# Layer 0's head norms: the Newton steps of a reciprocal square root, moved from VectorE to GpSimd

## The chip, the cores and the metric

The kernel runs on one core of a Trainium2 chip. A core has five engines that run side by side, each with its own in-order queue: TensorE (matrix products; PE in the profile, PEld for its weight loads), VectorE (DVE), ScalarE (ACT), GpSimd (POOL) and SyncE (SP, which here issues the loads). They wait for each other through semaphores. The metric is the time of one execution on the device in microseconds (us), lower is better.

## The reference, cut to what matters

Two transformer layers on 512 tokens of width 2048. Layer 0 is differential attention with 8 heads; layer 1 is another attention and has no head norm. What is computed around the change:

```python
o = from_blocks(lax.map(block, (to_blocks(q), jnp.arange(S // BLOCK))))   # (B, S, 8 heads, 256)
o = rms_norm(o, subln_g) * (1.0 - lam_init)
o = o.reshape(B, S, A_WIDTH) * jax.nn.silu(g)
return o @ w_out

def rms_norm(x, g):
    xf = x.astype(jnp.float32)
    y = xf * lax.rsqrt(jnp.mean(jnp.square(xf), axis=-1, keepdims=True) + EPS)
    return (y * g.astype(jnp.float32)).astype(x.dtype)
```

So each token of each head needs one reciprocal square root of its mean square over 256 values.

## The kernel before, in words

Activations and weights are fp32, held as a high part and a low part (`hh`/`hl`, `whi`/`wlo`); each product is three matmuls: L173 high x high, L174, L175 (with a low part). Weights stream from HBM into `wst`; ScalarE rounds a piece to `whi` (L93) and VectorE makes `wlo` (L94), some pieces ahead of use. A projection is a `group`: eight pieces of two 128-row tiles, each multiplied into four accumulator banks `acc`, so 24 matmuls per piece. A "burst" is six of these.

Attention of a head is cut into pieces, and one is issued after every burst of a projection (`tick`), so that TensorE has projection work while the vector engines work on the head. For layer 0 the attention of head h-1 runs beside the projections of head h. Its pieces, per block of 128 tokens i (0 to 3): two `score` (matmuls into `sc`; VectorE's L699 adds the bias and finds the row's extreme; ScalarE's exponential L703; VectorE's L707 to L711 combine both components into `e`), `turn` (TensorE transposes `e`, L720; the result is split into `ah` and `al`, L168 and L169), `values` (matmuls into `o`), and after every second `values` a `norm`, for two token blocks at once. `store` later transposes `og` on TensorE (L767), and ScalarE copies it out (L769). The order of pieces after the scores: values(1) with the first norm, score(3,0), turn(2), score(3,1), an empty one, values(2), store(0), turn(3), store(1), values(3) with the second norm, four empty ones, store(2), store(3). So a head has a first and a second norm, 16 norms in layer 0.

A norm: ScalarE copies `o` to `og` (L746) and sums the squares into `ss`, 128 tokens x 2 blocks (L749). VectorE scales `ss` (L750) and calls `rsqrt` on the 128x2 values: a first guess by integer operations (L246, L247, the latter writing `rstd`), the halved argument (L248), then three Newton steps of three instructions (L253, L254, L255). Then two instructions L753 multiply `og` by `rstd` and by the gate `sg`. `rsqrt` with n == 1 serves the layer norms, with two instructions a step (L251, L255). `rsqrt` with n == 2 is used by these 16 norms alone.

VectorE also carries, beside this, the sums of the modulation vectors: `macc` (L386), fed by loads `ms`, and turned into rows by two matmuls (L406, L407). At the end of a projection of values and gates it frees the accumulator banks (`vl`, L169, and `sg`, L675).

Only the start of the program has a written order. From there on a scheduler orders each engine's queue by its own estimates, so a changed instruction can move others. GpSimd has had little to do: the constants at the start, and `dist` (L646).

Of the kernel before, what the change touches and what calls it, by code (L numbers as in the profile page):

```python
# [13 lines left out]
ALU = mybir.AluOpType  # L14
# [95 lines left out]
def tile_yoco(  # L110
# [24 lines left out]
    V, S, PE, G = nc.vector, nc.scalar, nc.tensor, nc.gpsimd  # L135
# [105 lines left out]
    def rsqrt(y, v, n, pool):  # L241

        t = pool.tile([P, n], I32, name="rs_t", tag=f"rs_t{n}", bufs=2)
        a = pool.tile([P, n], F32, name="rs_a", tag=f"rs_a{n}", bufs=2)
        h = pool.tile([P, n], F32, name="rs_h", tag=f"rs_h{n}", bufs=2)
        V.tensor_scalar(t, v.bitcast(I32), 1, None, op0=ALU.logical_shift_right)  # L246
        V.tensor_scalar(y.bitcast(I32), t, -1.0, float(0x5F3759DF), op0=ALU.mult, op1=ALU.add)  # L247
        V.tensor_scalar(h, v, -0.5, None, op0=ALU.mult)  # L248
        for _ in range(3):
            if n == 1:  # L250
                V.scalar_tensor_tensor(a, y, h, y, op0=ALU.mult, op1=ALU.mult)  # L251
            else:
                V.tensor_tensor(a, y, y, op=ALU.mult)  # L253
                V.tensor_tensor(a, a, h, op=ALU.mult)  # L254
            V.scalar_tensor_tensor(y, a, 1.5, y, op0=ALU.add, op1=ALU.mult)  # L255


    ws = WeightStream(nc, wpool)
# [419 lines left out]
    def attention_a(h, lead=3, late=()):  # L678
# [62 lines left out]
        def norm(p):  # L741
            o = st["o", p]
            og = ap.tile([P, 2, 256], F32, name="og", tag="og", bufs=1)
            ss = ap.tile([P, 2], F32, name="ss", tag="ss", bufs=2)
            rstd = ap.tile([P, 2], F32, name="rstd", tag="rstd", bufs=2)
            S.copy(og.rearrange("p r e -> p (r e)"), o)  # L746
            for r in range(2):
                orow = o[:, r * 256 : (r + 1) * 256]
                S.activation(orow, orow, AF.Square, accum_out=ss[:, r : r + 1])  # L749
            V.tensor_scalar(ss, ss, 1.0 / 256.0, EPS, op0=ALU.mult, op1=ALU.add)  # L750
            rsqrt(rstd, ss, 2, ap)
            for r in range(2):
                V.scalar_tensor_tensor(  # L753
                    og[:, r, :], og[:, r, :], rstd[:, r : r + 1], cur[h, "sg"][:, 2 * p + r, :],
                    op0=ALU.mult, op1=ALU.mult,
                )
            st["og", p] = og
# [83 lines left out]
    def moments(pool, stats, b):  # L841
        mv = pool.tile([P, 2], F32, name="mv", tag="mv", bufs=4)
        V.bn_aggr(mv, stats[:, b, :, :])
        ve = pool.tile([P, 1], F32, name="lve", tag="lve", bufs=4)
        rstd = pool.tile([P, 1], F32, name="lrstd", tag="lrstd", bufs=4)
        V.tensor_scalar(ve, mv[:, 1:2], EPS, None, op0=ALU.add)
        rsqrt(rstd, ve, 1, pool)
        return mv, rstd
# [450 lines left out]
```

## Time and profile before

| | |
|---|---|
| median of 3 runs | 2016.16 us (2014.56 to 2017.47) |
| profiled execution | 2017.03 us, span of its profile 2015.2 us |
| mean granted TensorE clock | 0.995 |
| layer 0's norms | from 248 to 871 us |

The span is what lies between the first and the last instruction in the profile; the time of an execution is a little longer. Shares of busy time are means over stages with different limits. In lists of instructions each row has the start, the time taken, engine, line, operation, result and operands, form, and, in brackets, how long the engine sat idle before it and what released it. In a table of waits a row has the waiting engine and line, what it waited for, the total, the number of times and the longest. In the view of one tile a row has the shortest, median and longest time in ns.

### The profile page before, as it was taken

What the parts mean: (1) busy time and instruction counts of PE and PEld (TensorE: products, weight loads), DVE (VectorE), ACT (ScalarE), POOL (GpSimd) and SP (SyncE); (2) the same over time, 40 slices, a digit from 0 to 9 for tenths busy, and PEclk for the clock granted to TensorE, in tenths of its full rate; (3) what the DMA queues carried; (4) which work ended last, traced back from release to release, by engine and by line L of the source; (5) the groups of instructions that cost most, each with busy time, mean ns of one, the idle gap of its engine ahead of it and who ended that gap; (6) DMA issues with size and microseconds to landing.
All of it is one profiled execution on the core that took longest, in us unless ns stands there. A gap on an engine that the chain in (4) does not pass through costs nothing.

```text
span 2015.2 us, 25053 instructions
## 1 busy us (share of the span) xinstructions
PE 1966.7 (98%) x9115; PEld 1624.6 (81%) x9115; DVE 1334.4 (66%) x2435; ACT 722.3 (36%) x1230; POOL 2.2 (0%) x10
## 2 busy tenths in 40 slices
PE   5999999999999999999999999999999999999997
PEld 4888878888878888888878877888888888888885
DVE  7887878777667677753575666645455555576678
ACT  2423444433333334432273222224333333453232
POOL 0000000000000000000000000000000000000000
PEclk8999999999999999999999999999999999999998
DMA  9995755574556565552344878844233323333754
GB/s 342 346 314 149 238 174 162 166 222 156 190 166 210 160 225 178 162 165 94 115 144 135 268 252 260 259 123 129 90 104 95 104 90 104 95 117 93 259 191 177
DMA packets 263095, 353.79 MB, mean 176 GB/s; under 512 B 18022, under 2 KB 162556, under 8 KB 262204
## 3 DMA queue, kind: packets, MB, share of 16 engines
q1 hardware_dynamic: 260592, 347.99, 53.7%
q10 hardware_dynamic: 2380, 4.21, 0.6%
q8 instruction: 71, 1.16, 0.2%
q14 instruction: 52, 0.43, 0.1%
HBM read 339.47 MB, written 12.66 MB: 175 GB/s over the span
## 4 chain that ended last, share of the span: by engine, by line
PE 77%; DVE 10%; DMA 10%; issue 2%; ACT 1%; SPq 1%; DVEq 0%; ACTq 0%
PE acc L173 22%; PE acc L175 22%; PE acc L174 22%; DMA ms<-in_w_mod_dram 7%; DVE macc L386 3%; DVE wlo L94 2%; PE sc L173 2%; PE sc L174 2%; PE sc L175 1%; DMA ms<-in_kv_w_mod_dram 1%; PE o L175 1%; PE o L174 1%; PE o L173 1%; PE tr L1163 1%; DMA sms<-in_w_mod_dram 1%
## 5 line engine op out<-in xcount | busy, mean ns | idle before, releaser
L93 ACT CAST whi<-wst 128x1024 fp32r<-128x1024 f32 (+2 forms) x339 | 349.5, 1032 | 672.9 <-PE acc L175 281.6
L94 DVE TENSOR_TENSOR wlo<-wst,whi 128x1024 fp32r<-128x1024 f32 (+2 forms) x339 | 404.4, 1195 | 268.1 <-ACT whi L93 263.9
L173 PE MATMUL acc<-whi,hh 128*128 128x512 f32 x1252 | 492.6, 397 | 0.9 <-ACT hh L933 0.8
L174 PE MATMUL acc<-wlo,hh 128*128 128x512 f32 x1252 | 489.7, 391 | 2.6 <-DVE wlo L94 2.6
L175 PE MATMUL acc<-whi,hl 128*128 128x512 f32 x1252 | 488.1, 390 | 0.0
L173 PE MATMUL acc<-hh,whi 128*128 128x512 f32 x1184 | 468.5, 396 | 1.3 <-ACT vt L977 0.9
L175 PE MATMUL acc<-hh,wlo 128*128 128x512 f32 x1184 | 462.3, 390 | 2.0 <-DVE wlo L94 2.0
L174 PE MATMUL acc<-hl,whi 128*128 128x512 f32 x1184 | 461.7, 390 | 0.0
L386 DVE SCALAR_TENSOR_TENSOR macc<-ms,cact,macc 128x512 f32<-128x512 f32 x360 | 269.9, 750 | 128.4 <-DMA ms<-in_w_mod_dram 95.6
L175 PEld LDWEIGHTS acc<-whi,hl 128*128 128x128 f32 x1252 | 235.3, 188 | 50.8 <-DVE hl L934 0.3
L174 PEld LDWEIGHTS acc<-wlo,hh 128*128 128x128 f32 x1252 | 235.6, 188 | 47.8 <-DVE wlo L94 4.3
L173 PEld LDWEIGHTS acc<-whi,hh 128*128 128x128 f32 x1252 | 235.7, 188 | 46.8 <-ACT hh L933 1.2
L175 PEld LDWEIGHTS acc<-hh,wlo 128*128 128x128 f32 x1184 | 222.3, 188 | 52.2 <-DVE wlo L94 4.2
L173 PEld LDWEIGHTS acc<-hh,whi 128*128 128x128 f32 x1184 | 222.5, 188 | 45.7 <-ACT vt L977 1.7
L174 PEld LDWEIGHTS acc<-hl,whi 128*128 128x128 f32 x1184 | 222.6, 188 | 41.1
L476 DVE SCALAR_TENSOR_TENSOR sacc<-sms,cact,sacc 128x512 f32<-128x512 f32 (+1 forms) x127 | 89.5, 705 | 4.8 <-DMA sms<-in_w_mod_dram 1.2
L1152 ACT ACTIVATE eb<-eb,mnb 128x128 f32<-128x128 f32 (+1 forms) x64 | 36.1, 563 | 96.4 <-DVE mnb L1149 95.2
L703 ACT ACTIVATE e<-e,mn 128x128 f32<-128x128 f32 (+3 forms) x64 | 36.0, 563 | 89.5 <-DVE mn L699 88.7
L1149 DVE CUSTOM_DVE_ANT_0 eb<-sc,biasb 128x128 f32<-128x128 f32 (+1 forms) x64 | 31.3, 490 | 52.7 <-PE sc L175 52.7
L1167 DVE TENSOR_TENSOR pTl<-tr,pTh 128x128 fp32r<-128x128 f32 (+1 forms) x64 | 31.2, 487 | 26.5 <-ACT pTh L1166 26.2
L1166 ACT CAST pTh<-tr 128x128 fp32r<-128x128 f32 (+1 forms) x64 | 27.2, 424 | 43.6 <-PE tr L1163 43.1
L769 ACT ACTIVATE ogT<-tr,subg 128x128 f32<-128x128 f32 x64 | 20.0, 364 | 56.4 <-PE tr L767 56.4
(251 smaller groups left out, 1739.2 us busy)
## 6 DMA issues: line engine op xcount, KB each, us to landing
wst<-in_a_w_in_dram SPq DMA_DIRECT2D x240, 256.0 KB
ms<-in_w_mod_dram SPq DMA_DIRECT2D x64, 512.0 KB
ms<-in_kv_w_mod_dram SPq DMA_DIRECT2D x64, 512.0 KB
wst<-in_kv_w_dram SPq DMA_DIRECT2D x64, 512.0 KB
ms<-in_w_mod_dram SPq DMA_DIRECT2D x128, 256.0 KB
wst<-in_b_w_in_dram SPq DMA_DIRECT2D x128, 256.0 KB
sms<-in_w_mod_dram SPq DMA_DIRECT2D x56, 512.0 KB
wst<-in_b_w_out_dram SPq DMA_DIRECT2D x48, 512.0 KB
```

Source lines behind the costliest of these rows:

```text
L93: self.nc.scalar.copy(hi[:, :, :w], st[:, :, :w])
L94: self.nc.vector.tensor_tensor(lo[:, :, :w], st[:, :, :w], hi[:, :, :w].bitcast(F32), op=ALU.subtract)
L173: PE.matmul(dst, lhs[0], rhs[0], start=start, stop=False)
L174: PE.matmul(dst, lhs[0], rhs[1], start=False, stop=False)
L175: PE.matmul(dst, lhs[1], rhs[0], start=False, stop=stop)
L386: V.scalar_tensor_tensor(acc, w, cact[:, kt : kt + 1], acc, op0=ALU.mult, op1=ALU.add)
L476: V.scalar_tensor_tensor(acc, w, sc, acc, op0=ALU.mult, op1=ALU.add)
L703: S.activation(e[:, :w], e[:, :w], AF.Exp, bias=mn, scale=-1.0, accum_out=rs)
L1149: V.tensor_tensor_reduce(out=e[:, :w], in0=sc[:, :w], in1=bias[:, :w], scale=-1.0, scalar=3.0e38, op0=ALU.add, op1=ALU.min, accum_out=mn)
L1152: S.activation(e[:, :w], e[:, :w], AF.Exp, bias=mn, scale=-1.0, accum_out=rs)
L1166: S.copy(pTh[:, 0 : i + 1, ts], src)
L1167: V.tensor_tensor(pTl[:, 0 : i + 1, ts], src, pTh[:, 0 : i + 1, ts].bitcast(F32), op=ALU.subtract)
```

## The change

In `rsqrt`, where n is not 1, the Newton steps go to GpSimd. The fused last instruction of a step (add 1.5, multiply) becomes two, so a step has four instructions and a norm twelve, each waiting for the one before. The first guess and the halved argument stay on VectorE, and so do the two multiplications after the root. The root of the layer norms (n == 1) is as it was.

```diff
         for _ in range(3):
             if n == 1:
                 V.scalar_tensor_tensor(a, y, h, y, op0=ALU.mult, op1=ALU.mult)
+                V.scalar_tensor_tensor(y, a, 1.5, y, op0=ALU.add, op1=ALU.mult)
             else:
-                V.tensor_tensor(a, y, y, op=ALU.mult)
-                V.tensor_tensor(a, a, h, op=ALU.mult)
-            V.scalar_tensor_tensor(y, a, 1.5, y, op0=ALU.add, op1=ALU.mult)
+
+                G.tensor_tensor(a, y, y, op=ALU.mult)
+                G.tensor_tensor(a, a, h, op=ALU.mult)
+                G.tensor_scalar(a, a, 1.5, None, op0=ALU.add)
+                G.tensor_tensor(y, a, y, op=ALU.mult)
```

Lines behind this place have numbers three higher in the changed kernel.

On VectorE, head 0's first norm, the old order with - and the new with +, from the first guess on:

```order
 L247 TENSOR_SCALAR rstd<-rs_t 128x2
-L657 SCALAR_TENSOR_TENSOR q0l<-part,q0h 128x512
-L253 TENSOR_TENSOR rs_a<-rstd 128x2
+L660 SCALAR_TENSOR_TENSOR q0l<-part,q0h 128x512
 L169 TENSOR_TENSOR k0l<-part,k0h 128x512
-L254 TENSOR_TENSOR rs_a<-rs_a,rs_h 128x2
+L389 SCALAR_TENSOR_TENSOR macc<-ms,cact,macc 128x512
+L756 SCALAR_TENSOR_TENSOR og<-og,rstd,sg 128x256 x2
 L169 TENSOR_TENSOR al<-tr,ah 128x384
```

Here `og` moved: before, 13 other instructions stood between the guess and it, with the nine Newton instructions strewn among them; now three do, and `al`, the next scores and `wlo` follow it.

On VectorE, head 2's second norm, where nothing else stood between (before, from the guess on):

```order
L247 TENSOR_SCALAR rstd<-rs_t 128x2
L253 TENSOR_TENSOR rs_a<-rstd 128x2
L254 TENSOR_TENSOR rs_a<-rs_a,rs_h 128x2
L255 SCALAR_TENSOR_TENSOR rstd<-rs_a,rstd 128x2
L253 TENSOR_TENSOR rs_a<-rstd 128x2
L254 TENSOR_TENSOR rs_a<-rs_a,rs_h 128x2
L255 SCALAR_TENSOR_TENSOR rstd<-rs_a,rstd 128x2
L253 TENSOR_TENSOR rs_a<-rstd 128x2
L254 TENSOR_TENSOR rs_a<-rs_a,rs_h 128x2
L255 SCALAR_TENSOR_TENSOR rstd<-rs_a,rstd 128x2
L753 SCALAR_TENSOR_TENSOR og<-og,rstd,sg 128x256 x2
```

And the same place now:

```order
L247 TENSOR_SCALAR rstd<-rs_t 128x2
L756 SCALAR_TENSOR_TENSOR og<-og,rstd,sg 128x256 x2
L94 TENSOR_TENSOR wlo<-wst,whi 128x1024
L169 TENSOR_TENSOR vl<-acc,vh 128x256 x2
L678 SCALAR_TENSOR_TENSOR sg<-th,acc 128x256 x2
```

The nine instructions are gone, and `og`, which waits for GpSimd, is the next in the queue; the weight split and the freeing of the banks stand behind it as before.

On TensorE, head 1's second norm, the transposes of `og` in the first bursts after it, now:

```order
L173 MATMUL acc<-whi,hh 128x512
L174 MATMUL acc<-wlo,hh 128x512
L770 MATMUL tr<-ident,og 128x128 x2
L175 MATMUL acc<-whi,hl 128x512
L173 MATMUL acc<-whi,hh 128x512
L174 MATMUL acc<-wlo,hh 128x512
L175 MATMUL acc<-whi,hl 128x512
L770 MATMUL tr<-ident,og 128x128 x2
L173 MATMUL acc<-whi,hh 128x512
L174 MATMUL acc<-wlo,hh 128x512
L175 MATMUL acc<-whi,hl 128x512
```

Both pairs moved ahead of 15 matmuls that stood before them; before, the second pair was followed by one more burst's three matmuls and head 2's first score:

```order
L174 MATMUL acc<-wlo,hh 128x512
L767 MATMUL tr<-ident,og 128x128 x2
L175 MATMUL acc<-whi,hl 128x512
L173 MATMUL acc<-whi,hh 128x512
L174 MATMUL acc<-wlo,hh 128x512
L175 MATMUL acc<-whi,hl 128x512
L767 MATMUL tr<-ident,og 128x128 x2
L173 MATMUL acc<-whi,hh 128x512
L174 MATMUL acc<-wlo,hh 128x512
L175 MATMUL acc<-whi,hl 128x512
L173 MATMUL sc<-k0h,q0h 128x256
```

At head 0's and head 4's second norms they moved ahead by one burst or less. On TensorE nothing else moved but the two matmuls of a modulation row at head 1's second norm. SP's loads of heads 0 and 1 changed places among themselves.

## The prediction

> **What bounds the kernel now.** I read the page's busy times first, then the stage of the head norms by itself (240 to 880 us, columns as in the table of stages: span, then busy time and count for PE, PEld, DVE, ACT, POOL, the granted clock, the DMA share, GB/s), then what TensorE waited for in that stage.
>
> ```profile
> span 2015.2 us, 25053 instructions
> PE 1966.7 (98%) x9115; PEld 1624.6 (81%) x9115; DVE 1334.4 (66%) x2435; ACT 722.3 (36%) x1230; POOL 2.2 (0%) x10
> 240.00:880.00 640.00, 633.47 (x3002) 525.45 (x3001) 457.21 (x974) 251.98 (x513) 0.00 (x0) 1.00 0.57 181
> PE tr L767 <- DVE og L753: 4.4, 5, 1.3
> PE tr L767 <- DVE al L169: 0.9, 1, 0.9
> PE tr L720 <- DVE ss L750: 0.6, 1, 0.6
> ```
>
> TensorE bounds it. In the 640 us of this stage it idles 640 - 633.5 = 6.5 us, at a granted clock of 1.00; VectorE is busy 457 us, 71%. So less work on VectorE is worth nothing by itself. Only two things count: how early a result that TensorE waits for comes, and how long VectorE's queue stands. The last three rows name 5.9 of those 6.5 us, and the largest, 4.4 us in five waits, ends with `og`, the instruction fed by the root that is moved. They are at head 0's two norms, head 1's first, head 4's second and head 5's first. No row names a load: the order of the weight and modulation loads on SP's queue, which shifts a little in heads 0 and 1, I cost at nothing, covered by TensorE's 24-matmul steps per loaded piece. Were that cover gone, a load would appear among these waits.
>
> **What is removed.** Nine VectorE instructions per norm, 16 norms: 144.
>
> ```profile
> L94 DVE TENSOR_TENSOR wlo<-wst,whi 128x1024 fp32r<-128x1024 f32 (+2 forms) x339 | 404.4, 1195 | 268.1 <-ACT whi L93 263.9
> L253 DVE TENSOR_TENSOR rs_a<-rstd x48: 141/161/164, 250.2 to 869.8; 128x2 f32<-128x2 f32 x48
> 381.93 0.17 DVE L247 TENSOR_SCALAR rstd<-rs_t 128x2 int32<-128x2 int32 x1
> 383.98 0.88 DVE L753 SCALAR_TENSOR_TENSOR og<-og,rstd,sg 128x256 f32<-128x256 f32 x2
> 386.51 0.38 PE L767 MATMUL tr<-ident,og 128*128 128x128 f32 x2
> 386.78 0.75 DVE L675 SCALAR_TENSOR_TENSOR sg<-th,acc 128x256 f32<-128x256 f32 x2
> 388.27 0.48 PE L173 MATMUL acc<-hh,whi 128*128 128x512 f32 x1
> 389.05 0.40 PE L173 MATMUL acc<-hh,whi 128*128 128x512 f32 x1
> 389.74 0.39 PE L173 MATMUL acc<-hh,whi 128*128 128x512 f32 x1
> ```
>
> The first Newton line (L253) takes 0.16 us, the median of 48, and the other two the same. 144 x 0.16 = 23 us of VectorE busy time go; off TensorE's path, so worth 0. The timeline rows are head 2's second norm, where the nine run alone: from the end of L247 (382.10) to `og` (383.98) they take 1.88 us, about 0.2 each. The new chain has to be held against 1.88 us there, and against 5 to 7 us where other work was interleaved.
>
> **What is added.** Twelve GpSimd instructions per norm, each waiting for the one before, with a handover from VectorE and one back. No row shows such an instruction on GpSimd; the nearest are its start-up rows:
>
> ```profile
> 0.24 0.10 POOL L1286 MEMSET const-float32-0.0<- 128x1 f32 x1 [0.24 <-issue]
> 0.87 0.20 POOL L181 MEMSET ones<- 128x128 f32 x1
> 1.11 0.29 POOL masks.py:199 TENSOR_SCALAR_AFFINE_SELECT ident<-ident 128x128 f32<-128x128 f32 x1
> 1.35 0.52 POOL L183 MEMSET mask<- 128x512 f32 x1
> 1.94 0.29 POOL L184 TENSOR_SCALAR_AFFINE_SELECT mask<-mask 128x128 f32<-128x128 f32 x1
> ```
>
> An element costs (0.52 - 0.20) / 384 = 0.83 ns (the two memsets). The select, the only one here that reads SBUF, would with 2 columns instead of 128 take 0.29 - 126 x 0.00083 = 0.185 us. Its wait on the mask's memset cost 1.94 - 1.87 = 0.07 us. So a dependent step is about 0.255 us, and the chain, with one more handover, 12 x 0.255 + 0.07 = **3.1 us** from the end of L247 to `og`. Bounds: 0.10 (the smallest memset) + 0.04 (gap from 1.07 to 1.11) = 0.14 a step, chain 1.75 us; and the whole select, 0.29 + 0.07 = 0.36 a step, chain 4.4 us. I take 0.255, because the select is the nearest in kind and needs only its columns cut.
> [...]
>
> VectorE's queue is in order, so `og` holds everything behind it until GpSimd is done. Queued behind are the lower half of the probabilities (`al`), the score rows `e`, the weight split `wlo`, and at the end of a group `vl`/`sg`, which free the accumulator banks.
>
> **What comes back of the 4.4 us.** In all five places the chain of 3.1 us ends before TensorE wants `og`, so the 4.4 us go; then I look at what is late next. The scheduler has moved `og` ahead of instructions that stood before it.
>
> ```profile
> 249.48 0.16 DVE L247 TENSOR_SCALAR rstd<-rs_t 128x2 int32<-128x2 int32 x1
> 250.89 0.55 DVE L169 TENSOR_TENSOR al<-tr,ah 128x384 fp32r<-128x384 f32 x1
> 253.62 0.28 PE L175 MATMUL o<-vh,al 128*128 128x256 f32 x1
> 255.99 0.75 DVE L711 SCALAR_TENSOR_TENSOR e<-e,rsum 128x512 f32<-128x512 f32 x1
> 257.28 0.41 PE L767 MATMUL tr<-ident,og 128*128 128x128 f32 x2 [1.27 <-DVE og L753]
> 258.92 0.60 PE L720 MATMUL tr<-ident,e 128*128 128x128 f32 x4
> 315.66 0.15 DVE L247 TENSOR_SCALAR rstd<-rs_t 128x2 int32<-128x2 int32 x1
> 315.78 0.75 DVE L386 SCALAR_TENSOR_TENSOR macc<-ms,cact,macc 128x512 f32<-128x512 f32 x1
> 320.18 0.75 DVE L711 SCALAR_TENSOR_TENSOR e<-e,rsum 128x512 f32<-128x512 f32 x1
> 322.68 0.41 PE L767 MATMUL tr<-ident,og 128*128 128x128 f32 x2 [0.93 <-DVE og L753]
> 324.30 0.60 PE L720 MATMUL tr<-ident,e 128*128 128x128 f32 x4
> ```
>
> Head 0's first norm: `og` starts at 249.64 + 3.1 = 252.74, its two rows take 0.88, `al` now follows and ends at 254.15; TensorE wants it at 253.62: 0.5 us wait. From the end of `al` to the end of the last `e` took 5.3 us before, of which some 1.2 were Newton steps and a `macc` now elsewhere; so `e` ends at 258.3, and TensorE, without its old 1.27 us wait but with the new 0.5, wants it at 258.15: 0.15. Returned: 0.65 us.
> Head 1's first: `og` ends at 315.81 + 3.1 + 0.88 = 319.8. Before, from L247's end to the end of the last `e` (320.93) took 5.1 us. Of that `al` and two `macc` now stand ahead of `og` (about 0.5 + 1.3, each 0.08 less than its row because the next starts that early), seven Newton steps fall away (0.7), and `wlo` comes in (1.1): 3.7 us, so `e` ends at 323.5. TensorE wants it at 324.30 - 0.93 = 323.37. Returned: 0.1 us.
> At the other three more than 2 us of other work moves from ahead of `og` to behind it, and I see nothing of it that is wanted sooner than now: 0.
>
> **What gets worse elsewhere.**
>
> ```profile
> 331.84 0.17 DVE L247 TENSOR_SCALAR rstd<-rs_t 128x2 int32<-128x2 int32 x1
> 336.77 0.88 DVE L753 SCALAR_TENSOR_TENSOR og<-og,rstd,sg 128x256 f32<-128x256 f32 x2
> 337.41 0.41 PE L767 MATMUL tr<-ident,og 128*128 128x128 f32 x2
> 554.88 0.17 DVE L247 TENSOR_SCALAR rstd<-rs_t 128x2 int32<-128x2 int32 x1
> 567.68 0.75 DVE L386 SCALAR_TENSOR_TENSOR macc<-ms,cact,macc 128x512 f32<-128x512 f32 x1 [1.45 <-DMA ms<-in_kv_w_mod_dram]
> 570.23 0.44 PE L767 MATMUL tr<-ident,og 128*128 128x128 f32 x2 [0.91 <-DVE al L169]
> ```
>
> Head 1's second norm: TensorE's transposes of `og` now stand 15 matmuls earlier. Three matmuls of 512 columns go by in 389.74 - 389.05 = 0.69 us, so the transposes are wanted 15 x 0.23 = 3.4 us earlier, at 334.0. `og`'s first half is there at 332.01 + 3.1 + 0.48 (half of the pair of 0.88, rounded up) = 335.6. A new wait of **1.6 us**, the largest single term.
> Head 2's second norm: chain 3.1 against 1.88, so `og` and all behind it are 1.2 us later. The transposes have 386.51 - 384.46 = 2.05 us of slack, the bank freed by `sg` (first at 387.1) 1.15 us: returned 0.1. Heads 3 to 7's second norms have the same shape and either as much slack or idle time on VectorE behind them: 0.
> Head 4's first norm: from 554.88 on VectorE has no gap of any size until the 1.45 us before 567.68, and TensorE already waits 0.9 us for the `al` that follows it. VectorE comes out up to 1.1 us later (3.1 us chain less what the nine took and what is interleaved); that gap, on a load, can take some of it. I take half, 0.5 us.
>
> **Sum**, against the profiled execution's 2017.0 us: -4.4 + 0.65 + 0.1 + 1.6 + 0.1 + 0.5 = -1.4 us. That execution lies 0.9 us above the median of the runs, 2016.16; on that median the forecast is 2014.8, say **2015 us**: no change that a measurement of this kernel can tell, for which I take 0.2% (4 us, 2012.1 to 2020.2; the three runs of before differ by 2.9 us).
>
> **Rivals.**
> *The GpSimd step is long* (0.36 us or more; slower). From 3.1 us on, a microsecond more of chain is a microsecond at five places (the terms above, but for two heads' transposes with slack): at 4.4 us 5 x 1.3 = 6.5 us, and about 1 us more where the second norms' 2.05 us of slack ends. Net -1.4 + 7.5 = +6, that is 2022 us. It decides from a step of about 0.33 us. For it: the small rows of GpSimd say little of an instruction with two inputs. Against: the select reaches 0.36 only with all its 128 columns.
> *GpSimd is held up by VectorE.* If each Newton step had to let a running VectorE instruction with two SBUF inputs finish, the chain would stretch by the VectorE work between L247 and `og`:
>
> ```profile
> 249.55 0.68 DVE L657 SCALAR_TENSOR_TENSOR q0l<-part,q0h 128x512 fp32r<-128x512 f32 x1
> 250.22 0.68 DVE L169 TENSOR_TENSOR k0l<-part,k0h 128x512 fp32r<-128x512 f32 x1
> 332.59 0.42 DVE L169 TENSOR_TENSOR vl<-raw,vh 128x256 fp32r<-128x256 f32 x1
> ```
>
> Head 0's first norm: 0.68 + 0.68 + 0.75 = 2.1 us; head 1's first, two `macc`, 1.5; head 1's second, two `vl`, 0.8; together +4.4, and at head 4's second, with two `macc` as well but slack for some of it, about +0.7. Net -1.4 + 5.1 = +3.7: 2020 us, on the border of what can be told. Nothing in this trace shows two-input work on both engines at once. [...]
> *The step is short* (0.14 us; faster at most by a hair). Chain 1.75 us: head 1's second norm still waits 0.25 us, the rest returns nothing: -4.1 us, 2012 us. More than the 6.5 us of idle time cannot be won.
>
> **How the numbers follow.** Forecast (2013 to 2019 us) 0.50; long step 0.24, nearly all slower by over 0.2%; held up by VectorE 0.15, half of it beyond 0.2%; short step 0.08, half of it beyond; something not seen 0.03. Faster 0.08, same 0.58, slower 0.34. The range, 2012 to 2023 us, takes in the short step, the hold-up and the long step at its bound; the rest of the long step lies above.
>
> **What would show it.** In the profile after: GpSimd with 192 more instructions, starting about 0.25 us apart in a norm; VectorE idle before `og`, released by GpSimd, up to 3 us at each of the 16; TensorE's wait for `og` down from 4.4 us in five to about 1.6 us in one, at head 1's second norm; some 0.5 us waits for `al`; TensorE's idle time between 240 and 880 us about 5 us. Starts about 0.4 us apart, and new waits on `sg` or `og` in every head, would make me wrong by the first rival; starts stretched to the length of a `macc` only where VectorE is busy, by the second.

## The result and the profile after

The changed kernel takes 2038.6 us (median; 2037.6 to 2042.2), the kernel before, run beside it, 2016.8: a ratio of 1.0109, 95% interval 1.0087 to 1.0130. It is 22 us slower; the forecast was 2015, its range ended at 2023. The profiled execution took 2042.2 us with a span of 2040.4, 25.2 more than before. The page's head, then the stage of the head norms over the same window as before, and over a window that ends at the same matmuls (240 to 901 us now, 240 to 876 before):

```profile
span 2040.4 us, 25107 instructions
PE 1978.6 (97%) x9115; PEld 1632.5 (80%) x9115; DVE 1315.8 (64%) x2291; ACT 722.8 (35%) x1230; POOL 46.6 (2%) x202
240.00:880.00 640.00, 620.24 (x2884) 512.32 (x2884) 428.39 (x809) 241.27 (x490) 41.75 (x179) 0.98 0.55 175
240.00:901.00 661.00, 641.24 (x2991) 529.63 (x2991) 438.62 (x830) 249.93 (x510) 44.45 (x192) 0.98 0.55 174
```

The same row of before:

```profile
240.00:876.00 636.00, 629.47 (x2984) 522.16 (x2983) 455.28 (x971) 249.73 (x510) 0.00 (x0) 1.00 0.57 181
```

Some 24 of the 25 us are here, in two parts. TensorE idles 19.8 us instead of 6.5 (661 - 641.2 against 636 - 629.5): 13.3 us. And it is busy 641.2 us instead of 629.5, 11.8 us more, at a granted clock of 0.98 instead of 1.00. Of these 11.8 some 1.6 are seven matmuls more in the window (x2991 against x2984, 0.23 us each; the changed kernel was already 1.3 us late at 240 us), so about 10 us are the same matmuls taking longer. What TensorE waited for, with lines three higher than before:

```profile
PE tr L770 <- DVE og L756: 5.9, 2, 3.6
PE tr L770 <- DVE al L169: 4.9, 3, 3.1
PE tr L723 <- DVE e L714: 2.2, 1, 2.2
PE o L175 <- DVE al L169: 1.8, 1, 1.8
PE acc L173 <- DVE sg L678: 1.2, 2, 0.9
PE tr L770 <- DVE vl L169: 1.2, 1, 1.2
PE tr L770 <- DVE mrow L411: 1.1, 1, 1.1
```

Before, five waits for `og` made 4.4 us and none was over 1.3. Now two make 5.9, and four results that stand behind `og` in VectorE's queue (`al`, `e`, `sg`, `vl`) wait as well. Held against before at the same place in TensorE's queue (the transposes of `og` have themselves moved in heads 0 and 1), the delay is 1.4 us at head 0's first `store`, 9.1 after its last, 15.9 after head 1's last, 17.3 in head 3, 23.3 after head 4's last and 25.2 after head 7's. So nearly 20 us of it arise in heads 0, 1 and 4.

The GpSimd steps themselves are as forecast where nothing disturbs them. The view of the tile `rs_a` (shortest, median and longest in ns, and who waited for its instructions), then head 2's second norm:

```profile
L255 POOL TENSOR_TENSOR rs_a<-rstd x48: 193/193/677, 250.6 to 896.0; 128x2 f32<-128x2 f32 x48
L256 POOL TENSOR_TENSOR rs_a<-rs_a,rs_h x48: 194/195/1721, 251.2 to 896.2; 128x2 f32<-128x2 f32 x48
L257 POOL TENSOR_SCALAR rs_a<-rs_a x48: 212/213/1174, 251.8 to 896.5; 128x2 f32<-128x2 f32 x48
...
  DVE og L756: 43.3, 16
...
397.74 0.17 DVE L247 TENSOR_SCALAR rstd<-rs_t 128x2 int32<-128x2 int32 x1
397.99 0.19 POOL L255 TENSOR_TENSOR rs_a<-rstd 128x2 f32<-128x2 f32 x1 [12.41 <-DVE rstd L247]
398.26 0.20 POOL L256 TENSOR_TENSOR rs_a<-rs_a,rs_h 128x2 f32<-128x2 f32 x1
401.32 0.88 DVE L756 SCALAR_TENSOR_TENSOR og<-og,rstd,sg 128x256 f32<-128x256 f32 x2 [3.40 <-POOL rstd L258]
```

Steps start 0.27 to 0.30 us apart, and from the end of the guess (397.91) to `og` it is 3.41 us. Nine of the sixteen chains take that, to 0.01. The other seven take 3.6 to 5.0, and they lie where VectorE has work with two operands in SBUF between the guess and `og`. The longest maximum above is at head 0's second norm:

```profile
271.92 0.16 DVE L247 TENSOR_SCALAR rstd<-rs_t 128x2 int32<-128x2 int32 x1
272.32 0.74 DVE L389 SCALAR_TENSOR_TENSOR macc<-ms,cact,macc 128x512 f32<-128x512 f32 x1
272.53 1.72 POOL L256 TENSOR_TENSOR rs_a<-rs_a,rs_h 128x2 f32<-128x2 f32 x1
272.98 1.22 DVE L94 TENSOR_TENSOR wlo<-wst,whi 128x1024 fp32r<-128x1024 f32 x1
277.11 0.88 DVE L756 SCALAR_TENSOR_TENSOR og<-og,rstd,sg 128x256 f32<-128x256 f32 x2 [2.91 <-POOL rstd L258]
277.74 0.66 PE L770 MATMUL tr<-ident,og 128*128 128x128 f32 x2 [3.63 <-DVE og L756]
282.04 0.63 PE L175 MATMUL acc<-whi,hl 128*128 128x512 f32 x1
282.46 0.63 PE L173 MATMUL acc<-whi,hh 128*128 128x512 f32 x1
...
284.00 0.39 PE L174 MATMUL acc<-wlo,hh 128*128 128x512 f32 x1
284.23 0.39 PE L175 MATMUL acc<-whi,hl 128*128 128x512 f32 x1
```

Three things stand in these rows. L256, a 0.19 us instruction, takes 1.72 us and ends at 274.25, when `macc` and then `wlo` (both with two operands from SBUF) have ended, the second at 274.20. VectorE then stands 2.91 us at `og`, and TensorE 3.63. And after that gap the matmuls of 512 columns start 0.42 us apart until 283.7, and 0.23 apart from 284.0.

### The profile page after: what moved, and what is told of

The parts are those of the page before. It is cut to its first block, busy times and chain, and to the rows that moved or that the text cites. A ratio compares the mean times of both kernels' runs of the same rounds, so it can differ in the third digit from the quotient of the medians.

```text
span 2040.4 us, 25107 instructions
## 1 busy us (share of the span) xinstructions
PE 1978.6 (97%) x9115; PEld 1632.5 (80%) x9115; DVE 1315.8 (64%) x2291; ACT 722.8 (35%) x1230; POOL 46.6 (2%) x202
## 3 DMA queue, kind: packets, MB, share of 16 engines
q8 instruction: 71, 1.16, 0.2%
## 4 chain that ended last, share of the span: by engine, by line
PE 76%; DVE 10%; DMA 9%; issue 2%; POOL 1%; ACT 1%; SPq 1%; DVEq 0%; ACTq 0%; POOLq 0%
PE acc L173 22%; PE acc L175 21%; PE acc L174 21%; DMA ms<-in_w_mod_dram 7%; DVE macc L389 3%; DVE wlo L94 2%; PE sc L174 2%; PE sc L173 2%; PE sc L175 1%; DMA ms<-in_kv_w_mod_dram 1%; PE o L175 1%; PE o L174 1%; PE o L173 1%; PE tr L1166 1%; DMA sms<-in_w_mod_dram 1%
## 5 line engine op out<-in xcount | busy, mean ns | idle before, releaser
L756 DVE SCALAR_TENSOR_TENSOR og<-og,rstd,sg 128x256 f32<-128x256 f32 x32 | 14.1, 482 | 43.3 <-POOL rstd L258 43.3
```

## The experiments

The theory (T) to be tested: `og` at the head of VectorE's in-order queue waits for the chain on GpSimd, so `og` and all behind it come late; TensorE idles, and after long gaps its clock falls, which costs again. The rivals: R1, the scheduler's new order costs the time; R2, GpSimd and VectorE slow each other; R3, the lower clock is only a mark of the waits.

| kernel | median us | ratio to before, 95% interval |
|---|---|---|
| changed | 2038.6 | 1.0109 [1.0087, 1.0130] |
| one step on GpSimd | 2015.8 | 0.9996 [0.9985, 1.0006] |
| two steps on GpSimd | 2024.5 | 1.0035 [1.0025, 1.0046] |
| last step alone on GpSimd | 2021.1 | 1.0020 [1.0006, 1.0034] |
| four instructions a step, all VectorE | 2019.6 | 1.0011 [0.9999, 1.0024] |
| GpSimd in heads 0, 1, 4 | 2031.1 | 1.0062 [1.0040, 1.0084] |
| GpSimd in the other heads | 2021.9 | 1.0026 [1.0014, 1.0038] |
| `og` later, GpSimd | 2026.4 | 1.0040 [1.0027, 1.0053] |
| `og` later, VectorE | 2016.8 | 0.9999 [0.9989, 1.0009] |
| `og` later, GpSimd at first norms | 2014.5 | 0.9985 [0.9973, 0.9996] |
| TensorE filled | 2039.8 | 1.0116 [1.0094, 1.0138] |
| gap probe, 12 | 2035.6 | 1.0091 [1.0065, 1.0118] |
| gap probe, 20 | 2049.2 | 1.0163 [1.0144, 1.0183] |
| eight writes and one step | 2021.4 | 1.0019 [1.0010, 1.0029] |

### The order or the chain: one step, two steps

```diff
-        for _ in range(3):
+        for _ in range(3 if n == 1 else 1):     # two_step_g: else 2
```

> The changed kernel with one Newton step on GpSimd instead of three (two steps of the root are left out, so the root is coarser). The order of the instructions stays nearly that of the changed kernel; the chain on GpSimd shrinks from about 3.3 us (4.5 to 5.0 where it is held up) to about 1.3. Theory T (VectorE's queue stands behind og until GpSimd is done, so og and what follows it come late; TensorE then idles, and its granted clock drops after the long gaps): the waits go, TensorE idles 5 to 8 us between 240 and 880 us as before, clock 1.00 there, time 2012 to 2018 us. Rival R1 (the new order that the scheduler chose costs the time, whatever the chain's length): 2030 us or more. If the time falls by a third of the loss only, a cost per handover is at work.

> The changed kernel with two Newton steps on GpSimd instead of three (one step of the root is left out). The chain is 1.1 us shorter than with three. Theory T with gaps that lower the clock only when long: TensorE's seven waits of 1.2 to 3.6 us shrink by 1.1 each, to about 8 us in all, one of them at most over 2 us, so little or no clock loss: 2020 to 2026 us, less than two thirds of the way from one step (2016) to three (2039). If the loss goes evenly with the chain's length: 2027 us or more.

With one step the kernel is as fast as before, at nearly the changed kernel's order (its transposes of `og` stand within three rows of the places they have there): R1 falls, and so does a cost per handover. The chain from guess to `og` is 1.16 us there where undisturbed. The stage of the norms in it, against 633.5 before:

```profile
240.00:880.00 640.00, 632.58 (x2994) 524.05 (x2993) 438.55 (x829) 251.19 (x513) 14.46 (x64) 1.00 0.57 181
```

Two steps (chain 2.28 us where undisturbed, up to 3.24 elsewhere) cost 7 us, three 22: by the ratios the second step costs about 8 us and the third 15. That agrees with T's growth, though not strongly.

### Where it arises

```diff
-            rsqrt(rstd, ss, 2, ap)
+            rsqrt(rstd, ss, 2, ap, h in (0, 1, 4))   # heads_rest: not in; others on VectorE
```

> The Newton steps on GpSimd in heads 0, 1 and 4 alone, the complement of the run with the other five heads, which lost 4 of the 22 us. Theory T: the long waits and the clock's falls all come back: 2032 to 2038 us. If the two parts don't add up (a loss that needs all 16 norms): 2028 us or less.

> The Newton steps on GpSimd in heads 2, 3, 5, 6 and 7 alone; heads 0, 1 and 4 as before. In the changed kernel TensorE's waits of over 1.2 us all lie in heads 0, 1 and 4, where a burst of TensorE's queue wants og, al or e soon, and where loads of the modulation fill VectorE. Theory T: 2017 to 2023 us (the waits of 1.1 us at heads 2 and 6 stay). If every norm on GpSimd costs alike, ten of sixteen norms give 10/16 of the 22 us: 2030 us.

The six norms of heads 0, 1 and 4 hold 12.5 us of the loss (ratio 1.0062), the ten others 5 (1.0026). The first is a microsecond under the expected range. The two sum to 0.9% of 1.1%, equal within the intervals. So the ten norms to which the forecast gave 0.1 us do cost, half a microsecond each, and a norm in heads 0, 1 and 4 costs four times that.

### Four instructions, and a short stand of VectorE

```diff
-                G.tensor_tensor(a, y, y, op=ALU.mult)        # and the three after it
+                V.tensor_tensor(a, y, y, op=ALU.mult)        # split_dve: all four on V
+                E = G if step == 2 else V                    # last_step: E for all four
```

> The changed kernel's four separate instructions a step, all on VectorE: 48 more VectorE instructions of 0.16 us than before, no GpSimd. It parts the split of the fused instruction from the engine. Theory T: 3 to 4 more instructions of about 0.2 us per norm on VectorE, 0.6 us later og at the places where TensorE waits: 2016 to 2021 us. If the split is what costs: 2025 us or more.

> Steps 1 and 2 of the root on VectorE (four separate instructions each), only the third step on GpSimd: one handover there and one back as in the changed kernel, four GpSimd instructions instead of twelve. The chain from guess to og where it runs alone: about 8 x 0.2 + 1.3 = 2.9 us. og's place in the order goes back to about that of before, with other work between the steps. Theory T: the standing of VectorE's queue is 1.3 us instead of 3.3 and more, a small loss: 2017 to 2024 us. If every handover to GpSimd and back costs TensorE time, whatever the chain: 2028 us or more.

The split of the fused instruction alone is not told from no change. With the last step on GpSimd besides, the kernel is 0.2% slower than before, inside what T expected: VectorE stands there 1.2 us at most, no gap of TensorE in the stage of the norms is over 1.8 us, and the clock stays at 1.00 there. From the split alone (0.11%) this run is not told apart, since the two intervals overlap.

### VectorE's stand taken away

```diff
         def norm(p):
-            for r in range(2): V.scalar_tensor_tensor(og..., rstd..., sg...)
+        def scale(p):    # a piece of its own
+            with tc.issue_after(st["last"].ins):     # the last e of the scores
+                for r in range(2): V.scalar_tensor_tensor(og..., rstd..., sg...)
-   score(3, 1), None, values(2), ... values(3), None, None, None, None, store(2), ...
+   score(3, 1), scale(0), values(2), ... values(3), None, None, scale(1), None, store(2), ...
```

> The changed kernel with the two multiplications of og taken out of the norm and issued as a piece of their own: at first norms after the last e of the second half of the scores, so VectorE does al, e and wlo while GpSimd works; at second norms three pieces later in the list, which moves the queue's order there little. Chain and GpSimd work are unchanged. Theory T: the waits at first norms (al 3.1 us at 591.8, e 2.2 us at 334.7, al 1.8 and 1.4 us in heads 0) go with their share of the clock drops; those at second norms (og 3.6 and 2.3 us) stay: 2020 to 2030 us. Rival R2 (VectorE's and GpSimd's instructions slow each other, whoever stands in the queue): 2034 us or more, since VectorE now works on while GpSimd does.

> The kernel before (Newton steps on VectorE) with og's two multiplications as a piece of their own, as in the run that deferred them with the steps on GpSimd. It is the control for that run: its order without GpSimd. If the deferral by itself costs or brings nothing: 2013 to 2019 us, and the 8 to 10 us by which the other lay above before are GpSimd's chain at the second norms. If the deferral itself costs: 2022 us or more.

> The deferral of og's multiplications with the Newton steps on GpSimd at the first norm of each head only; the second norms' steps are on VectorE. At first norms VectorE then never stands behind og while GpSimd works, though GpSimd's chain is longer there (6 us and more, held up by VectorE's work). Theory T (the cost is VectorE's standing and og's lateness, not GpSimd's work): 2013 to 2020 us, as with all steps on VectorE. Rival R2 (GpSimd's work beside VectorE's slows VectorE and costs by itself): 2022 us or more.

With all roots on GpSimd 14 of the 22 us go, by the ratios. What stays is mostly at the second norms, where little is put between: 6.2 of the 8.7 us in the first row are the waits for `og` in heads 0 and 1 there (3.92 and 2.30). With the second norms' roots on VectorE too (third row: its stage of the norms) the loss is gone:

```profile
PE tr L777 <- DVE og L763: 8.7, 5, 3.9
254.25 1.09 POOL L258 TENSOR_TENSOR rstd<-rs_a,rstd 128x2 f32<-128x2 f32 x1
```

```profile
240.00:880.00 640.00, 635.11 (x3008) 526.53 (x3007) 451.35 (x905) 252.25 (x513) 33.44 (x96) 1.00 0.57 182
```

In both kernels GpSimd's chain at head 0's first norm is 7 us long, since VectorE goes on working beside it and holds up its steps (the row at 254.25, of the first of the two, shows one of 1.09 us), and it costs nothing: R2 falls as a cost by itself. The last kernel, 2014.5 us, is the only one whose whole interval lies below 1, by 0.15%; that is less than the 0.2% that can be told from no change. With the steps on VectorE the same deferral brings nothing that can be told (0.9999), but the two intervals overlap, so whether the last kernel gains anything stays open.

### The clock

```diff
+   fill({(0, 2): 13, (1, 2): 10, (4, 1): 13}.get((h, i), 0))   # in store; 10 more in turn(3) of head 1
```

> The changed kernel with 46 matmuls more on TensorE, written to a scores bank that nobody reads, put ahead of the four places where TensorE waited longest (heads 0 and 1 second norms, head 4 first, head 1's last turn). At 0.23 us each they are 10.5 us of work that fits into the waits or, where it doesn't, is added. If the clock drop is a consequence of the gaps and costs time of its own (theory T): the granted clock in 240 to 880 us is 0.99 to 1.00 and the time falls to 2026 to 2032 us although work was added. Rival R3 (the clock drop is a mark of the waits in the profile and costs nothing of its own): 2037 to 2042 us.

Missed as to time: T's 2026 to 2032 did not come. Of the 10.5 us of matmuls the waits hid less than half: in the profile TensorE idles 4.9 us less than in the changed kernel up to 901 us. At head 0 it did what was meant, at head 1 one of two gaps stayed (2.22 us), at head 4 the gap only moved on to the next transposes:

```profile
277.67 0.44 PE L779 MATMUL tr<-ident,og 128*128 128x128 f32 x2 [1.42 <-ACT ogT L781]
600.10 0.66 PE L779 MATMUL tr<-ident,og 128*128 128x128 f32 x2 [3.78 <-DVE og L764]
```

The 3.63 us gap is gone, a wait of 1.42 stands at the next transposes, the clock does not fall (1.00 from 276 to 288 us), and head 0's last transposes start at 277.7 instead of 280.8, with 3 us of work more. After the 3.78 us gap it falls again (0.50 from 600 to 604 us). By the total this run decides nothing; TensorE's busy time on its page leans to T, since it is only 2.9 us above the changed kernel's (1981.5 against 1978.6) with 10.5 us of matmuls more. So gaps were made on purpose, in the kernel before:

```diff
+            if p == 1 and h in (2, 3, 5, 6, 7):
+                late = st["late"] = ap.tile([P, 2], F32, ...)
+                G.tensor_scalar(late, rstd, 1.0, None, op0=ALU.mult)
+                for _ in range(11): G.tensor_scalar(late, late, 1.0, ...)   # gap_20: 19
         def store(i):
+                if i == 2 and "late" in st: PE.transpose(sc_bank("gap")[0:2, 0:P], st["late"], ident)
```

> The kernel before (roots on VectorE), with a chain of 12 small GpSimd instructions, fed by the root, at the second norms of heads 2, 3, 5, 6 and 7, and one small transpose of its result on TensorE just ahead of og's transposes. Only TensorE waits for this chain; VectorE never does. At 0.29 us a step it ends some 3.5 us after the root; in head 2 TensorE stood 2.6 us behind the root, so five gaps of about 1 us. Theory T (a gap costs its length, and below about 2 us nothing more): clock 1.00 in 240 to 880 us, time 2020 to 2024 us. Rival R3 gives the same here; the pair with 20 instructions tells them apart.

> As with 12 instructions, the chain now of 20: same order on TensorE, only the chain is 2.3 us longer, so five gaps of about 3.3 us, 16 us in all. Theory T (a gap of over 2 us makes the granted clock fall, which costs 1.7 to 3.4 us more at each): time 2040 to 2050 us, clock about 0.98 in 240 to 880 us. Rival R3 (the lower clock in the profile costs nothing of its own): 2031 to 2036 us.

The page's busy times with 12 steps, the waits for this chain, the clock of the stage, and two of the chains:

```profile
PE 1972.6 (97%) x9120; PEld 1628.3 (80%) x9120; DVE 1334.7 (66%) x2435; ACT 722.8 (36%) x1230; POOL 25.8 (1%) x70
PE gap L770 <- POOL late L756: 14.3, 5, 4.5
240.00:880.00 640.00, 622.47 (x2927) 515.23 (x2926) 449.09 (x952) 244.35 (x497) 19.48 (x48) 0.99 0.55 176
383.81 4.17 POOL L756 TENSOR_SCALAR late<-late 128x2 f32<-128x2 f32 x11
479.89 5.96 POOL L756 TENSOR_SCALAR late<-late 128x2 f32<-128x2 f32 x11
```

And with 20, with the matmuls behind the longest gap:

```profile
PE 1975.5 (97%) x9120; PEld 1631.9 (80%) x9120; DVE 1334.4 (65%) x2435; ACT 722.7 (35%) x1230; POOL 34.4 (2%) x110
240.00:880.00 640.00, 613.40 (x2867) 507.69 (x2866) 441.98 (x933) 240.02 (x488) 26.28 (x80) 0.98 0.54 174
491.58 0.37 PE L770 MATMUL gap<-ident,late 128*2 128x128 f32 x1 [6.91 <-POOL late L756]
492.60 0.63 PE L174 MATMUL acc<-wlo,hh 128*128 128x512 f32 x1
493.03 0.63 PE L175 MATMUL acc<-whi,hl 128*128 128x512 f32 x1
...
496.24 0.39 PE L173 MATMUL acc<-whi,hh 128*128 128x512 f32 x1
496.47 0.40 PE L174 MATMUL acc<-wlo,hh 128*128 128x512 f32 x1
```

With 12 steps the expectation missed by 12 us: the gaps are not about 1 us but 1.81, 1.82 and 2.11, and 4.55 and 4.02 in heads 3 and 6, where the chain was held up longest (5.96 us for eleven steps against 4.17). The clock fell after just these two (behind the one of 4.02 matmuls started 0.43 us apart, behind the one of 2.11 at 0.23). With 20 the gaps are 4.2 to 6.9, and the clock fell at all five. Its time is in the expected range partly by luck, since the gaps are 26 us in all and not 16. The spans are 2033.1 and 2046.1 us, 17.9 and 30.9 longer than before (2015.2), and by the pages TensorE is busy 5.9 and 8.8 us longer than before (1966.7), for five small transposes more: that much of the loss is not idle time, while VectorE did its work as before (1334.4 us busy). The rows show it directly: 0.43 us from one matmul to the next behind the gap, 0.23 a few microseconds later. R3 falls, though the two medians alone (13.5 us apart, 11.8 of them longer gaps) would not have decided it.

How far the clock falls stands in the changed kernel's profile: at its four falls the granted clock reads 0.50, for 6.8 us from 276.9, 3.4 from 334.9, 3.4 from 348.6 and 6.8 from 590.9. By these readings TensorE's busy time is 9.4 us longer there (3.0, 1.7, 1.7 and 3.0), which is the "about 10 us" above, and 0.43 against 0.23 us from matmul to matmul agrees with it. How long a gap must be, the runs do not settle: of the gaps from 1.7 to 3.1 us in the stage of the norms 7 of 18 came with a fall in the profiles of this study, of those from 3.6 us all 11.

### The hold-up on GpSimd

```diff
+        if n == 2:                               # tw: the tile of t, now 64 columns wide
+            a = t.bitcast(F32)
+            for _ in range(8): G.memset(tw.bitcast(F32), 0.0)   # starts when the guess has read t
-        for _ in range(3):
+        for _ in range(3 if n == 1 else 1):
```

> The changed kernel with twelve GpSimd instructions per norm as there, but the first eight are memsets (128x64, on the guess's work tile, so they start when the guess is done) and only the last four are a Newton step; two steps of the root are left out. The order on TensorE and VectorE is that of the changed kernel but for og at two places, which stands one row further back. A memset reads no SBUF. The clean chain, 3.4 us in the changed kernel, should be 2.8 to 3.4 us. Port theory (a GpSimd instruction that reads SBUF is blocked while VectorE reads two SBUF operands): the chains of 4.5, 5.0 and 4.5 us in heads 0 and 1 come down to the clean length, since VectorE's work is over when the four readers start; TensorE's wait of 3.6 us at head 0's second norm falls under 2 us and the clock there stays at 1.00; time 2022 to 2032 us. If any work of GpSimd is stretched by VectorE, written or read: chains of 4.5 us and more again at these places, 2034 us or more. If the stretch is there but costs little: chains clean, and 2034 us or more.

The tile's row, and the same place as above, head 0's second norm:

```profile
L253 POOL MEMSET rs_t<- x128: 151/151/154, 250.5 to 877.4; 128x64 f32 x128
...
270.69 1.61 POOL L253 MEMSET rs_t<- 128x64 f32 x8 [17.48 <-DVE rstd L248]
270.87 0.74 DVE L394 SCALAR_TENSOR_TENSOR macc<-ms,cact,macc 128x512 f32<-128x512 f32 x1
271.53 1.22 DVE L94 TENSOR_TENSOR wlo<-wst,whi 128x1024 fp32r<-128x1024 f32 x1
272.38 0.42 POOL L260 TENSOR_TENSOR rs_t<-rstd 128x2 f32<-128x2 f32 x1
273.69 0.88 DVE L761 SCALAR_TENSOR_TENSOR og<-og,rstd,sg 128x256 f32<-128x256 f32 x2 [0.94 <-POOL rstd L263]
```

128 memsets, none over 154 ns, right beside `macc` and `wlo`; the one reader that meets the rest of `wlo` takes 0.42 and ends (272.80) when `wlo` does (272.75). The chain here is 3.07 us instead of 5.03, in heads 0 and 1 otherwise 2.84 to 2.90, and the time is 2021.4, half a microsecond under the expected range. So it is reads of SBUF that are held up. The changed kernel's own chains show which work of VectorE does it: beside `al`, `mrow` and `e`, which take one operand from PSUM (TensorE's result memory), five chains in heads 2, 3, 4 and 6 kept their 3.41 us, and only beside work with both operands in SBUF were steps stretched (to as much as 1.72 us, from 0.19). The expectation names a port; the runs show the hold-up alone, not what lies behind it. The clean chain is also 0.57 us shorter than the changed kernel's, so not all of the 17 us between the two is the hold-up. Two steps, with a clean chain shorter still by 0.56 us but with readers that are held up, take 3 us more than this kernel (1.0035 against 1.0019). That points to some 3 us at least for the hold-up, but the two intervals overlap a little, and how the 17 us divide stays open.

## Why the prediction was wrong, point by point

**The bound and the removed work: right.** TensorE is still the bound, and 19 us less of VectorE busy time (23 were reckoned) are worth nothing.

**The chain of 3.1 us: nearly right where undisturbed (3.41, at 0.27 to 0.30 a step against 0.255), wrong in the places that count.** At heads 0 and 1 it was 4.49, 5.03, 4.46 and 3.59. The second rival had the hold-up, at the right instructions (`q0l`, `k0l`, `macc`), with stretches of 2.1 and 1.5 us where 1.1 were measured; it got a chance of 0.15, for want of a row with both engines at work, though this change makes just that overlap. It missed head 0's second norm, the worst (1.6 us): `macc` and `wlo` stood between guess and `og` there before, and one of each stays there, but the prediction counted at that norm only the work that moves behind `og`. And its price (2020 us) went by idle time alone.

**"Returned: 0.65 us" at head 0's first norm:** 1.75 for `al` and 0.13 for `e`, where 0.5 and 0.15 were reckoned. The hold-up and the longer step, 1.4 us on the chain, cover that difference; the working held. No term had the wait of 1.40 that follows at 265.87, where the next transposes of `og` need the bank that the next `al` empties. **"Returned: 0.1" at head 1's first:** 2.22, of which 1.36 is the chain (4.46 against 3.1); the rest is VectorE's work behind `og`, 0.2 longer than reckoned, and TensorE, there some 0.4 sooner after the guess. **"1.6 us, the largest single term", head 1's second:** 2.28; the hold-up and the step were 0.5 more.

**"At the other three ... 0": the step that failed most.** Head 0's second norm was thought gained; it became the longest wait, 3.63 us. `og` came 0.55 us sooner after the guess than before (5.03 against 5.58), but TensorE wanted it 3.5 us sooner: its transposes had moved up by 7 rows (1.6 us), which the order showed and I passed over as "one burst or less" (a burst is six), and the guess itself came later beside TensorE.

**"I take half, 0.5 us", head 4's first:** TensorE's wait went from 0.91 to 3.06.

```profile
577.84 0.88 DVE L756 SCALAR_TENSOR_TENSOR og<-og,rstd,sg 128x256 f32<-128x256 f32 x2 [2.22 <-POOL rstd L258]
589.27 0.75 DVE L389 SCALAR_TENSOR_TENSOR macc<-ms,cact,macc 128x512 f32<-128x512 f32 x1 [2.11 <-DMA ms<-in_kv_w_mod_dram]
591.08 0.69 DVE L169 TENSOR_TENSOR al<-tr,ah 128x512 fp32r<-128x512 f32 x1
591.82 0.69 PE L770 MATMUL tr<-ident,og 128*128 128x128 f32 x2 [3.06 <-DVE al L169]
```

VectorE stood 2.22 us at `og` and came out at that load 12.73 us after the guess instead of 11.18, so 1.55 us later and not 1.1. And the gap at the load, which should have taken some of it up, grew from 1.45 to 2.11: a load that waits for a buffer to be freed by late work comes late with it (inferred from these rows). No slack was there.

**"Heads 3 to 7's second norms ... 0", and head 2's 0.1:** 1.17 for `vl` in head 2, 1.11 for `mrow` in head 6, 0.9 for `sg`; the run with heads 2, 3, 5, 6 and 7 alone shows 5 us. Small waits, all of the kind foreseen.

**The missing term: the clock.** About 10 of the 25 us are matmuls at a lower clock (granted 0.50) behind gaps of 2.2 to 3.6 us. The profile before showed 1.00 throughout, with no gap over 1.3 us in this stage, so it had no row to price this from; but every term here was a new gap, and that a microsecond of it costs a microsecond ("a microsecond more of chain is a microsecond at five places") was taken as given. Any chance for waits as long as these should have carried an extra cost, and the range a longer upper end.

**What would show it:** GpSimd's 192 instructions and VectorE's stand (43.3 us in 16, longest 3.4) came as written. TensorE's waits did not: 5.9 us for `og` in two instead of 1.6 in one, and 19.8 us of idle time instead of about 5. "Starts stretched ... only where VectorE is busy" named the second rival's sign, and that is what the profile shows.

## What to carry to other kernels

Moving a short dependent chain to an idle engine frees nothing if the in-order engine that it came from must wait for the result next: take the consumer out of that queue's way first (with that done at the first norms, GpSimd's chain of 7 us cost nothing). Before giving GpSimd work that reads SBUF, look at what VectorE runs in the same microseconds: what ran there with two operands in SBUF stretched the chain (at head 0's second norm `macc` and `wlo` made it 5.03 us instead of 3.41). And when a change opens gaps on TensorE, they can cost more than their length: here 13 us more of idle time came with about 10 us of slower matmuls, and behind a gap of 2.22 us the granted clock stood at 0.50 for 3.4 us.

## What had not been expected of the hardware

- After a gap TensorE's matmuls of 512 columns started 0.43 us apart instead of 0.23, for several microseconds (in the changed kernel the granted clock read 0.50 for 3.4 or 6.8 us each time). In the stage of the norms gaps of 3.6 us and more always did it (11 of 11), one of 1.75 us once did, and one of 3.02 us did not.
- A GpSimd instruction that reads SBUF can be held through two VectorE instructions in a row: 1.72 us for one of 0.19, through `macc` and `wlo`. GpSimd got no turn between them.
- GpSimd's memsets beside the same work never took more than 154 ns (median 151).
